# Where the vector work of a gated linear attention stage stands in its plan: mixes, gate sums, one scaling and one norm factor moved

## The chip, the cores and the metric

The kernel runs on one core of one Trainium2 chip, in one launch. The metric is the device time of that launch in microseconds (us), lower is better. The kernel computes with TensorE (PE, matrix products), VectorE (DVE), ScalarE (ACT), GpSimd (POOL) and the queue of SyncE (SP), which starts most of the transfers from memory. Each engine works through its own instructions in a fixed order and waits where an operand or a buffer is not there yet.

## The reference

Two layers over 512 positions of width 1024, all in float32. The first layer mixes by pooling and a short convolution, the second by gated linear attention; each is followed by a gated FFN with a convolution. The change lies in the attention of the second layer alone:

```python
q, k, v, r, gl = jnp.split(h, [...], axis=-1)              # h = rmsnorm(x) @ gla_w_in
g = jax.nn.log_sigmoid((gl @ w_g2 + b_g).astype(f32)) / GLA_TAU
bcum = jnp.cumsum(heads(g, GLA_HK), axis=3)                # in chunks of 64 positions
q_in = q * jnp.exp(bcum);  k_in = k * jnp.exp(-bcum)
att = jnp.where(mask, jnp.einsum('bhnlk,bhnmk->bhnlm', q_in, k_in), 0.0)
o_intra = jnp.einsum('bhnlm,bhnmv->bhnlv', att, v)
kv = jnp.einsum('bhnlk,bhnlv->bhnkv', k * jnp.exp(b_last - bcum), v)
_, states = lax.scan(step, init, (kv, decay))              # state over the chunks
o = o_intra + jnp.einsum('bhnlk,bhnkv->bhnlv', q_in, states)
o = o * lax.rsqrt(jnp.mean(o * o, axis=-1, keepdims=True) + EPS) * norm_g
o = o.reshape(bsz, s, GLA_DV) * jax.nn.silu(r)             # then @ gla_w_out, + x
```

There are four heads, with 128 columns of q and k and 256 of v and r each.

## The kernel before

**Number format.** Every matrix product is taken in three parts: each float32 operand is split into a high part (ACT copies it to a shorter format) and a low part (DVE subtracts), and PE adds high by high, high by low and low by high. So each block of weights costs a transfer into a `raw` buffer (three of them), an ACT instruction (`hi`, line 219) and a DVE instruction (`lo`, line 223) before PE can use it.

**The plan.** The attention stage is one list of steps. `at(t, fn)` puts a step at a planned time; `run_plan` sorts the steps by time and emits them, and PE, DVE and ACT then keep exactly that order. The planned times are not enforced at run time: they only set the order of each engine's queue. Transfers on SP and POOL wait for their buffers.

**The buffers.** Products land in PSUM, which has eight banks of 128x512; a bank is handed out when the program is built, and a product whose bank is still being read waits. Intermediate tiles of 128x512 come from a pool of 41 slots (`slot`).

The stage runs as follows; `t` is the planned time.

1. **v and the low-rank gate input**: `v_chunk` (lines 1063 to 1065, tile `vg`) takes the token-major products, four column blocks b = 0 to 3 with four banks each, and `v_out` (line 1069) copies each bank out. Beside b = 0 the row norm is found: `rsqrt_small` takes `v` (line 294), `y` (296), `t` (300, 301) and the result `y` (302), which the spreading product `bc` (line 328) needs on PE. Beside b = 1 the gate input is transposed (`low_rank`, `glT`), and `gate_logits` (lines 1009, 1011, tile `z`) follow: heads 0 and 1 ahead of b = 2, heads 2 and 3 in the middle of it. `log_gate`, `log_gate2` (ACT: exp and log) and `log_gate3` (DVE: line 1027 and the running sum, line 1029, tile `bc`) make the gate sums of all heads.
2. **The mixes** (`mix_parts`, `mix_in_plan`), four of them, also lie beside v. They build sums of the two halves of x for a seven-product scheme that the q and k projections use: ACT scales (`scale`, line 420), DVE takes four sums (`sums`, lines 427 to 430), ACT makes two high parts (`high`, line 435), DVE two low parts (`low`, line 440).
3. **Pairs of r and q/k**, for heads 0 to 3: `gate(i)` is the projection of r in six parts of four products (line 1274, tile `r`), then scaled by DVE (line 391) and put through Silu by ACT (line 1340). `queries_keys(h)` takes seven products p1, p2, p6, p5, p7, p3, p4 of twelve matmuls (line 562) into three banks: `stx`, `styz`, `stz`. ACT copies `stx` out between them (`keep`, line 1306), and p6 has to wait for the copy of p1's result. The piece `a2` of the weights that p3 and p4 use is split beside the products (lines 513 and 519).
4. **Head by head**: `decays` and `decays2`, `decays3` need the gate sum; `keys`, `keys2` scale q and k; `scores` (banks `att`, `kot`), `masked`, `kv`, `states` (ACT line 1143, DVE line 1145), `outputs` (two banks `o` per head, lines 1155 and 1157).
5. **Norm of a head**: `squares_of` squares both `o` banks (ACT, line 1166), adds (DVE, line 1169) and splits the sum (`nh`, ACT line 315; `nl`, DVE line 316). `head_norm` puts the total over the partitions on PE (lines 311 and 312, tile `ss`) and `out_norm` the steps after it: ACT `ny` and `nt` (318, 319), DVE `nt` (320), ACT `nt` (321), DVE `ro` (322), and the scaling `y` of both halves (line 1185), which reads the two `o` banks for the last time.
6. **Output**: `out_gate` multiplies with Silu(r) (line 1195) and splits (`yh`, ACT line 1199; `yl`, DVE line 1203). Then `mix_out` takes the output projection (line 264, tile `go`). It is not in the plan: its first two blocks start with the parts of heads 0 to 2, and the rest needs head 3's. Each of its results is added to x (line 347) and prepared for the FFN; this uses a `raw` buffer too (`xg`), so that the sixth block of weights of `go` waits for it.

r's eight projections stand at: gate(0) ahead of the first q/k pair, gate(1) to gate(3) ahead of the next, gate(4) to gate(7) behind the last, with the outputs of heads 2 and 3 between them.

Of the kernel before, what the change touches and what calls it, by code (L numbers as in the profile page):

```python
# [72 lines left out]
def trunk_kernel(ctx, tc, xT, cols, w_ab, w_pool, w_abo, w_vg, w_qk, w_r, w_g2, w_go, w_up, w_dn, w_ds, outT):  # L73
# [11 lines left out]
    def slot(dt=F32, name="s"):  # L85
        return big.tile([P, T], dt, tag="s", name=name)
# [27 lines left out]
    def col(name, i=0):  # L114
        c = COLS[name] + i
        return colt[:, c : c + 1]
# [48 lines left out]
    def f32(ap):  # L165
        return ap.bitcast(F32)
# [76 lines left out]
    done = [0]  # L243
# [81 lines left out]
    def spread_small(y, n):  # L325
        b = bank("bc")[:, : n * P]
        for c in range(n):
            PE.matmul(
                b[:, c * P : (c + 1) * P], y[:, c : c + 1].broadcast_to([P, P]), ident, start=True, stop=True
            )  # L330
        return b

    def sums(acc, c0=0, n=NTT):
        b = bank("ss")
        for c in range(n):
            PE.matmul(b[:, c : c + 1], acc[:, (c0 + c) * P : (c0 + c + 1) * P], ones[:, 0:1], start=True, stop=True)
        return b
# [121 lines left out]
    def at(t, fn):  # L459
        events.append((t, len(events), fn))  # L460
# [487 lines left out]
    total = []  # L948
# [76 lines left out]
    def log_gate3(h):  # L1025
        e, z = heads[h].pop("e"), heads[h].pop("z")
        V.scalar_tensor_tensor(z, z, 0.0, e, ALU.min, ALU.subtract)
        bc = heads[h]["bc"] = slot(name="bc")
        V.tensor_tensor_scan(bc, starts, z, 0.0, ALU.mult, ALU.add)
# [130 lines left out]
    def squares_of(h, t):  # L1160
        q = heads[h]

        def raw():
            q["sq"] = [slot(name="osq") for _ in range(2)]
            for sq, o in zip(q["sq"], q["o"]):
                S.activation(sq, o, AF.Square)

        def total():
            V.tensor_tensor(q["sq"][0], q["sq"][0], q["sq"][1], ALU.add)
            q["ro"], q["norm"] = norm_wide(q["sq"][0], 256, "ro")  # L1170

        at(t, raw)
        at(t + 1.3, total)
        ready_at = 6.5 if h < 2 else 1.7
        at(t + ready_at, lambda: q["norm"][0]())
        at(t + ready_at + (1.6 if h < 2 else 0.6), lambda: q["norm"][1]())

    def out_norm(h, t):
        q = heads[h]
        for step, after in zip(range(3, 8), (0.0, 0.7, 1.4, 2.2, 3.0)):  # L1180
            at(t + after, lambda step=step: q["norm"][step]())

        def scale(e):
            q.setdefault("y", []).append(slot(name="y"))
            V.scalar_tensor_tensor(q["y"][e], q["o"][e], col("gnorm", e), q["ro"], ALU.mult, ALU.mult)

        for e in range(2):
            at(t + 3.8 + 0.7 * e, lambda e=e: scale(e))

    def out_gate(h, e, t):  # L1190
        i = 2 * h + e

        def gate():
            y = heads[h]["y"][e]
            V.tensor_tensor(y, y, sil[i], ALU.mult)

        def high():
            y_h[i] = slot(F32R, "yh")
            S.activation(y_h[i], heads[h]["y"][e], AF.Copy)

        def low():
            y_l[i] = slot(F32R, "yl")
            V.tensor_tensor(y_l[i], heads[h]["y"][e], f32(y_h[i]), ALU.subtract)

        at(t, gate)
        at(t + 0.8, high)
        at(t + 1.5, low)

    def mix_in_plan(i, t):
        scale, sums, high, low = mix_parts(i, "mix1")  # L1210

        def done():
            mixed[i] = low()

        at(t, scale)
        at(t + 0.8, sums)
        at(t + 2.2, high)
        at(t + 3.5, done)

    t = 0.0  # L1220

    def then(us, fn):
        nonlocal t
        at(t, fn)
        t += us

    def next_block(lead=13.0, high=8.0, low=6.6):
        block(t - lead, t - high, t - low)
# [4 lines left out]
    at(0.0, lambda: V.tensor_scalar(minus_gain, colt[:, COLS["mix1"] + HK : COLS["mix1"] + KD], -1.0, None, ALU.mult))  # L1233
    mixed = [None] * HK
    for i in range(HK):
        mix_in_plan(i, 9.6 + 4.6 * i)
    first = True
    for b, (n, ks) in enumerate(zip(VG_COLS, VG_K)):
        k0 = 0
        for i, kt in enumerate(ks):  # L1240
            if b or i > 1:
                next_block()
            then(kt * 12 * n * 0.000443, lambda b=b, n=n, k0=k0, kt=kt: v_chunk(b, n, k0, kt))
            k0 += kt
            if b == 0 and i == 1:
                then(0.9, lambda: rsqrt_small(y4, sums(acc)[:, :NTT], NTT, D))
            if b == 0 and i == 2:
                then(0.9, lambda: S.activation(rs, spread_small(y4, NTT), AF.Copy))
            if b == 1 and i == 0:
                then(0.5, low_rank)  # L1250
            if (b, i) in ((1, 1), (2, 0)):
                for h in ((0, 1) if b == 1 else (2, 3)):
                    then(0.24, lambda h=h: gate_logits(h))
                    at(t + 1.5, lambda h=h: gate_sizes(h))
            if b == 2 and i == 0:
                for h in range(HEADS):
                    at(t + 2.2 + 0.1 * h, lambda h=h: log_gate(h))
                    at(t + 4.6 + 0.1 * h, lambda h=h: log_gate2(h))
                    at(t + 6.0 + 2.0 * h, lambda h=h: log_gate3(h))
        for c in range(NTT):  # L1260
            at(t + 0.1 + 0.4 * c, lambda b=b, n=n, c=c: v_out(b, n, c))

    scaled_at, sil_at = {}, {}
# [24 lines left out]
    def queries_keys(h):  # L1288
        nonlocal t
        w = seven_weights(w_qk[h], t, "gla", 2)  # L1290
        b, q = {}, {}

        def product(name):
            if not qk_ops:
                qk_ops.update(operands(mixed))
            out, first, ts = {
                "p1": ("x", True, lo_t), "p2": ("yz", True, lo_t), "p6": ("x", False, lo_t),
                "p5": ("z", True, lo_t), "p7": ("x", False, lo_t), "p3": ("yz", False, hi_t),
                "p4": ("x", False, lo_t),
            }[name]  # L1300
            seven_product(w, b, qk_ops, name, out, first, ts)

        def keep(tile, ts):
            if tile not in q:
                q[tile] = slot(name=tile)
            S.activation(q[tile][:, ts], b["x"][:, lo_t], AF.Copy)

        def add_p5(tile):
            V.tensor_tensor(q[tile][:, hi_t], b["z"][:, lo_t], q[tile][:, hi_t], ALU.add)

        def key():
            V.scalar_tensor_tensor(q["k"], q["k"], -1.0, rs, ALU.mult, ALU.mult)
            heads[h]["k"] = q["k"]

        def query():
            V.tensor_tensor(q["q"], b["yz"], q["q"], ALU.add)

        def query2():
            V.tensor_tensor(q["q"], q["q"], rs, ALU.mult)
            heads[h]["q"] = q["q"]  # L1320

        for n, name in enumerate(DOWN_SEVEN):
            at(t + n * UNIT, lambda name=name: product(name))
        at(t + 1 * UNIT + 0.1, lambda: keep("q", lo_t))
        at(t + 3 * UNIT + 0.1, lambda: keep("q", hi_t))
        at(t + 4 * UNIT + 0.2, lambda: add_p5("q"))
        at(t + 5 * UNIT + 0.1, lambda: keep("k", hi_t))
        at(t + 5 * UNIT + 0.6, lambda: add_p5("k"))
        t += 7 * UNIT
        at(t - 0.6, query)  # L1330
        at(t + 0.1, lambda: keep("k", lo_t))
        at(t + 0.15, query2)
        at(t + 0.8, key)
# [4 lines left out]
    def gate(i, between={}, split_at=(6.0, 4.8)):  # L1338
        project_into("r", i, store_r, between, split_at)
        at(t + 1.2, lambda: S.activation(sil[i], sil[i], AF.Silu))  # L1340
        sil_at[i] = t + 1.8
# [18 lines left out]
    def head_norm(h):  # L1360
        then(0.46, lambda: heads[h]["norm"][2]())
        out_norm(h, t + 0.1)
        scaled_at[h] = t + 5.4

    def gates_of(h, t):
        at(t + 2.0, lambda: decays(h))
        at(t + 1.6, lambda: decays2(h))
        at(t + 5.8, lambda: decays3(h))

    gate(0)  # L1370
    gates_of(0, t)
    queries_keys(0)
    head_keys(0, 1.6)
    gate(1, {4: lambda: head_scores(0)}, (3.6, 2.4))
    gates_of(1, t)
    queries_keys(1)
    head_kv(0)
    head_keys(1, 1.6)
# [9 lines left out]
    late = t + 2.5  # L1388
# [5 lines left out]
    head_scores(3)  # L1394
    gate(5, {4: lambda: (head_kv(3), head_norm(2))})
    gate(6, {1: lambda: head_out(3)})
    gate(7, {4: lambda: head_norm(3)})
    for h in range(HEADS):
        for e in range(2):
            out_gate(h, e, max(scaled_at[h] + 0.7 * e, sil_at[2 * h + e], late + 5.0 + 8.0 * h + 0.7 * e if h < 2 else 0.0))  # L1400
    for i in range(2):
        block(t - 8.0 + 3 * i, t - 5.0 + 2.5 * i, t - 3.8 + 2.5 * i)
    run_plan()
# [141 lines left out]
```

## Time and profile before

| | |
|---|---|
| three runs, median | 1012.91 us (1012.45 to 1013.28) |
| the profiled execution | 1013.42 us |
| its span, first to last instruction | 1011.7 us |
| mean granted TensorE clock | 0.997 |
| busy in the span: PE, DVE, ACT, POOL | 998.2, 847.1, 623.6, 69.6 us |
| the attention stage, by the timeline of PE | from 467.98 (first `vg`) to 628.42 (first `go`) |
| the output projection `go` | 628.42 to 673.48 |

In a timeline each row has the start, the time to the end of the last instruction of the row, the engine, the line, the operation, output and inputs with their shape, and the number of instructions; a bracket gives the time that the engine sat idle before it (from about 0.15 us up) and whom it waited for. Starts are in us from the start of the span. Consecutive instructions overlap a little, so the distance of two starts is shorter than the duration of the first: a DVE step of 128x512 lasts 0.69 us and takes 0.60 us of the queue.

### The profile page before, as it was taken

The numbers are of one execution on the slowest core, as the hardware profiler recorded it, in microseconds if no ns is written. First come the engines' busy times: TensorE is split into PE (matmuls) and PEld (weight loads), VectorE is DVE, ScalarE is ACT, GpSimd is POOL, SyncE is SP. The second block draws the span as 40 slices with busy tenths as digits, with TensorE's granted clock in tenths as the row PEclk, the third lists the DMA queues.
The fourth block names the chain that finished last, engine by engine and source line by source line (L and its number), as shares of the span: only waits on it lengthen the run. The fifth ranks groups of instructions, "written<-read, shape, count | busy, mean of one in ns | idle before, by whom it ended". The sixth has DMA issues, their size and how long they took to land.

```text
span 1011.7 us, 17531 instructions
## 1 busy us (share of the span) xinstructions
PE 998.2 (99%) x6996; PEld 925.4 (91%) x6996; DVE 847.1 (84%) x1224; ACT 623.6 (62%) x954; POOL 69.6 (7%) x93
## 2 busy tenths in 40 slices
PE   9999999999999999999999999999999999999996
PEld 7888889999999988899999998789999999988896
DVE  7886689999999997767868787789999999997775
ACT  6442567766766754345785767767766766764451
POOL 0001000111111000002000000100101101000000
PEclk9999999999999999999999999999999999999998
DMA  6437136787787454527325112736687787454522
GB/s 223 147 103 179 54 111 166 194 204 182 198 205 183 129 130 135 142 76 199 103 79 140 53 67 80 188 115 170 184 207 184 197 202 184 137 125 133 135 87 84
DMA packets 61267, 147.03 MB, mean 145 GB/s; under 512 B 5152, under 2 KB 7584, under 8 KB 61184
## 3 DMA queue, kind: packets, MB, share of 16 engines
q1 hardware_dynamic: 45808, 116.93, 36.2%
q0 software_dynamic: 14688, 28.32, 17.3%
q8 instruction: 55, 0.90, 0.3%
q10 hardware_dynamic: 688, 0.65, 0.2%
q14 instruction: 28, 0.23, 0.1%
HBM read 143.78 MB, written 2.10 MB: 144 GB/s over the span
## 4 chain that ended last, share of the span: by engine, by line
PE 89%; DVE 5%; ACT 4%; DMA 1%; issue 1%; SPq 0%; DVEq 0%; ACTq 0%
PE stx L562 29%; PE styz L562 18%; PE dn L264 15%; PE abo L264 4%; PE pc L264 2%; PE dn L562 2%; PE pb L264 2%; PE px L264 2%; PE go L264 2%; PE r L1274 2%; PE stz L562 2%; PE v L596 1%; PE u L596 1%; PE pu L264 1%; PE vg L1063 1%; PE vg L1065 1%
## 5 line engine op out<-in xcount | busy, mean ns | idle before, releaser
L519 DVE TENSOR_TENSOR lo<-raw,hi 128x1024 fp32r<-128x1024 f32 x108 | 131.9, 1222 | 17.4 <-ACT hi L513 17.4
L513 ACT ACTIVATE hi<-raw 128x1024 fp32r<-128x1024 f32 x108 | 114.3, 1059 | 22.5 <-PE styz L562 15.1
L223 DVE TENSOR_TENSOR lo<-raw,hi 128x1024 fp32r<-128x1024 f32 (+3 forms) x83 | 95.9, 1157 | 17.6 <-ACT hi L219 16.9
L219 ACT ACTIVATE hi<-raw 128x1024 fp32r<-128x1024 f32 (+3 forms) x83 | 83.2, 1002 | 19.2 <-DMA raw<-in_w_ab 4.8
L495 POOL DMA_DIRECT2D s<-in_w_up x42 | 50.7, 1206 | 577.4 <-ACT k L614 136.0
L380 DVE SCALAR_TENSOR_TENSOR cacc<-u,colt,cacc 128x511 f32<-128x511 f32 x96 | 71.6, 746 | 1.8 <-ACT cacc L377 1.8
L377 ACT ACTIVATE cacc<-u,colt 128x512 f32<-128x512 f32 x48 | 39.4, 821 | 45.9 <-DVE u L629 36.1
L519 DVE TENSOR_TENSOR lo<-s,hi 128x1024 fp32r<-128x1024 f32 x54 | 65.7, 1217 | 0.0
L513 ACT ACTIVATE hi<-s 128x1024 fp32r<-128x1024 f32 x54 | 57.2, 1059 | 1.1
L562 PE MATMUL stx<-th,hi 128*128 128x256 f32 x368 | 56.7, 276 | 0.0
L562 PE MATMUL stx<-th,lo 128*128 128x256 f32 x368 | 56.7, 276 | 0.0
L562 PE MATMUL stx<-tl,hi 128*128 128x256 f32 x368 | 56.7, 276 | 0.0
L264 PE MATMUL dn<-mh,hi 128*128 128x512 f32 (+1 forms) x238 | 56.5, 377 | 0.0
L264 PE MATMUL dn<-mh,lo 128*128 128x512 f32 (+1 forms) x238 | 56.4, 376 | 0.0
L264 PE MATMUL dn<-ml,hi 128*128 128x512 f32 (+1 forms) x238 | 56.4, 376 | 0.0
L562 PE MATMUL styz<-xh,lo 128*128 128x256 f32 x360 | 55.4, 276 | 0.0
L562 PE MATMUL styz<-xh,hi 128*128 128x256 f32 x360 | 55.4, 276 | 0.0
L562 PE MATMUL styz<-xl,hi 128*128 128x256 f32 x360 | 55.4, 276 | 0.0
L264 PEld LDWEIGHTS dn<-mh,lo 128*128 128x128 f32 x238 | 42.9, 188 | 8.2
L513 ACT ACTIVATE sh<-raw 128x512 fp32r<-128x512 f32 x54 | 34.3, 635 | 26.1 <-DVE raw L524 26.1
L264 PEld LDWEIGHTS dn<-ml,hi 128*128 128x128 f32 x238 | 42.9, 188 | 8.2
L264 PEld LDWEIGHTS dn<-mh,hi 128*128 128x128 f32 x238 | 42.2, 188 | 7.7
(347 smaller groups left out, 2612.8 us busy)
## 6 DMA issues: line engine op xcount, KB each, us to landing
raw<-in_w_up SPq DMA_DIRECT2D x46, 512.0 KB, 6.2
s<-in_w_up SPq DMA_DIRECT2D x42, 512.0 KB, 6.8
s<-in_w_up POOLq DMA_DIRECT2D x42, 512.0 KB, 6.4
raw<-in_w_dn SPq DMA_DIRECT2D x32, 448.0 KB, 3.3
raw<-in_w_up SPq DMA_DIRECT2D x42, 256.0 KB, 3.2
raw<-in_w_ab SPq DMA_DIRECT2D x14, 512.0 KB, 3.5
raw<-in_w_abo SPq DMA_DIRECT2D x8, 512.0 KB, 4.0
s<-in_w_ds SPq DMA_DIRECT2D x8, 512.0 KB, 6.2
```

The source lines that it names most:

```text
L219: S.activation(parts[0], raw, AF.Copy)
L223: V.tensor_tensor(parts[1], raw, f32(parts[0]), ALU.subtract)
L264: PE.matmul(out, w[:, k, :], a[k], start=first and i == 0 and k == 0, stop=last and i == 2 and k == n - 1, skip_group_check=loose,)
L377: S.activation(acc[0], u, AF.Identity, bias=col(bname, j), scale=col(wname, 2 * nj + j))
L380: V.scalar_tensor_tensor(a, u[:, : T - i], col(wname, (2 - i) * nj + j), a, ALU.mult, ALU.add)
L495: G.dma_start(w["s31"].rearrange("p (a n) -> p a n", a=2), part, accum_op=ALU.add)
L513: S.activation(h, src(), AF.Copy)
L519: V.tensor_tensor(lo, src(), f32(h), ALU.subtract)
L562: PE.matmul(b[out][:, ts], wt[:, ks[k]], a[k], start=first and i == 0 and k == 0, stop=i == 2 and k == HK - 1, skip_group_check=True,)
L596: PE.matmul(o, w[:, k, :], a[k], start=i == 0 and k == 0, stop=i == 2 and k == KD - 1)
L1063: PE.matmul(o[c][:, :n], xh[kk][:, cs], h[:, k, :], start=kk == 0, stop=False)
L1274: PE.matmul(o, w[:, k, :], a[k], start=i == 0 and k == 0, stop=k == KD - 1 and i == 5, skip_group_check=True)
```

## The change

Only planned times are altered, and with them the order in which the engines get the steps. No instruction is added, removed or altered.

- **Mixes**: the four mixes start at 7.0, 11.6, 21.0 and 25.6 in place of 9.6, 14.2, 18.8 and 23.4; inside a mix the high parts come 0.8 later and the low parts 0.7 later. In DVE's order the sums of mix 0 now stand ahead of `rsqrt_small`, the low parts of mix 0 and the sums of mix 1 ahead of the third weights block's `lo`; only the sums of mix 2 stand between `glT` and the `z` of heads 0 and 1, and mix 3's sums and low parts come behind these.
- **Gate sums**: `log_gate3` of heads 2 and 3 leaves the stretch beside b = 3. Head 2's goes behind the `decays` of head 0, ahead of `a2`'s low part in the first q/k pair; head 3's goes between the two `add_p5` of the second pair.
- **Head 0's scaling**: the step `ro` and both `y` of head 0 go 13.0 later, from among the `keys` of head 2 into the fourth q/k pair: `ro` ahead of head 1's `nl`, the first `y` ahead of `a2`'s low part, the second between the two `add_p5`.
- **Head 3's norm**: its sum and split come earlier behind its squares, its total on PE goes from behind part 4 to behind part 1 of gate(7), and with it all steps up to `yh` and `yl`. The split of gate(7)'s weights goes 4.0 earlier (on ACT ahead of head 3's `states`, on DVE behind them), and head 2's `out_gate` 4.0 later (behind head 3's `nl`).

```diff
-        at(t + 1.3, total)
-        ready_at = 6.5 if h < 2 else 1.7
+        at(t + (0.6 if h == 3 else 1.3), total)
+        ready_at = (6.5, 6.5, 1.7, 0.8)[h]
...
     def out_norm(h, t):
         q = heads[h]
-        for step, after in zip(range(3, 8), (0.0, 0.7, 1.4, 2.2, 3.0)):
+        late = 13.0 if h == 0 else 0.0
+        for step, after in zip(range(3, 8), (0.0, 0.7, 1.4, 2.2, 3.0 + late)):
...
-            at(t + 3.8 + 0.7 * e, lambda e=e: scale(e))
+            at(t + 3.8 + late + 0.7 * e, lambda e=e: scale(e))
...
-        at(t + 2.2, high)
-        at(t + 3.5, done)
+        at(t + 3.0, high)
+        at(t + 4.2, done)
...
-        mix_in_plan(i, 9.6 + 4.6 * i)
+        mix_in_plan(i, (7.0, 11.6, 21.0, 25.6)[i])
...
-                    at(t + 6.0 + 2.0 * h, lambda h=h: log_gate3(h))
+                    if h < 2:
+                        at(t + 6.0 + 2.0 * h, lambda h=h: log_gate3(h))
...
     gates_of(0, t)
+    at(t + 4.9, lambda: log_gate3(2))
...
     gates_of(1, t)
+    at(t + 7.3, lambda: log_gate3(3))
...
-    gate(7, {4: lambda: head_norm(3)})
+    gate(7, {1: lambda: head_norm(3)}, (10.0, 8.6))
...
-            out_gate(h, e, max(scaled_at[h] + 0.7 * e, sil_at[2 * h + e], ...))
+            out_gate(h, e, max(scaled_at[h] + 0.7 * e + 4.0 * (h == 2), sil_at[2 * h + e], ...))
```

More of the change, by code (lines that the diff above doesn't have):

```diff
@@ L1396, in trunk_kernel @@
     gate(6, {1: lambda: head_out(3)})
-    gate(7, {4: lambda: head_norm(3)})
+    gate(7, {1: lambda: head_norm(3)}, (10.0, 8.6))
     for h in range(HEADS):
         for e in range(2):
-            out_gate(h, e, max(scaled_at[h] + 0.7 * e, sil_at[2 * h + e], late + 5.0 + 8.0 * h + 0.7 * e if h < 2 else 0.0))
+            out_gate(h, e, max(scaled_at[h] + 0.7 * e + 4.0 * (h == 2), sil_at[2 * h + e], late + 5.0 + 8.0 * h + 0.7 * e if h < 2 else 0.0))
     for i in range(2):
```

## The prediction

> **What bounds the kernel now.** I read the page first, then the busy time by stretches of the attention stage, then the timeline of PE there for rows with a bracket, then the timelines of DVE and ACT around each of these.
>
> ```profile
> span 1011.7 us, 17531 instructions
> PE 998.2 (99%) x6996; PEld 925.4 (91%) x6996; DVE 847.1 (84%) x1224; ACT 623.6 (62%) x954; POOL 69.6 (7%) x93
> ...
> 468.00:517.00 49.00, 48.06 (x409) 47.68 (x408) 35.01 (x59) 34.95 (x57) 5.13 (x15) 1.00 0.44 121
> ...
> 571.00:594.00 23.00, 22.42 (x166) 20.98 (x166) 18.69 (x33) 16.55 (x25) 0.00 (x0) 1.00 0.19 63
> ...
> 629.00:674.00 45.00, 44.06 (x194) 35.80 (x193) 36.26 (x53) 32.47 (x46) 3.62 (x3) 1.00 0.62 164
> ```
>
> PE is busy for 99% of the span, and the change takes no matmul away. So only time in which PE waits can be won, and only in this stage: 49.00 - 48.06 = 0.94, 0.58 and 0.94 us in three stretches (length, then PE's busy time). The granted clock (third number from the end) is 1.00 in all of them. PE's timeline shows these 2.5 us as four waits:
>
> ```profile
> 498.80 0.39 PE L1063 MATMUL vg<-hi,xh 128*128 128x256 f32 x1 [0.94 <-DVE z L1011]
> 587.00 0.74 PE L562 MATMUL stx<-th,sh 128*128 128x256 f32 x4 [0.58 <-ACT q L1306]
> 639.82 1.19 PE L264 MATMUL go<-yh,hi 128*128 128x512 f32 x4 [0.36 <-ACT yh L1199]
> 657.02 2.11 PE L264 MATMUL go<-yh,hi 128*128 128x512 f32 x8 [0.58 <-ACT hi L219]
> ```
>
> Their sum is 0.94 + 0.58 + 0.36 + 0.58 = 2.46 us, 0.24% of the time. That is the most that the change can win, apart from losses too short for a bracket. Everything else is what it adds.
>
> **Mixes, the wait at 498.80.** PE needs a bank that the DVE step `z` frees; `z` stood late in DVE's queue.
>
> ```profile
> 478.43 0.15 DVE L294 TENSOR_SCALAR v<-ss 128x4 f32<-128x4 f32 x1
> ...
> 479.30 0.16 DVE L302 SCALAR_TENSOR_TENSOR y<-t,y 128x4 f32<-128x4 f32 x1
> 479.52 0.43 DVE L427 TENSOR_TENSOR ta<-xg 128x256 f32<-128x256 f32 x1
> ...
> 481.17 1.22 DVE L223 TENSOR_TENSOR lo<-raw,hi 128x1024 fp32r<-128x1024 f32 x1
> ...
> 495.08 0.43 DVE L427 TENSOR_TENSOR ta<-xg 128x256 f32<-128x256 f32 x1 [0.87 <-ACT xg L420]
> ...
> 497.99 1.41 DVE L1011 TENSOR_SCALAR z<-z,colt 128x512 f32<-128x512 f32 x2
> ...
> 480.88 1.05 PE L328 MATMUL bc<-ident,y 128*128 128x128 f32 x8
> ```
>
> Ahead of `z` stand the sums of mix 3 (from 495.08, 1.65 as below), an idle 0.87, and mix 2's two low parts (about 1.2). All of these leave, 3.7 us; `z` starts near 494.3, as soon as its product is there. The wait lasts 0.94, so it goes: **-0.94**.
>
> The price lies at the other end. The sums of mix 0 now stand ahead of `v`. Four sums take 479.52 to 481.17 = 1.65 us. The result `y` (L302) ended at 479.30 + 0.16 = 479.46 and now ends at 481.11. PE's spreading product `bc` started at 480.88 without a wait. From the end of `z` (497.99 plus half of 1.41 = 498.70) to the matmul that it released (498.80) is a hand-over of 0.10. So `bc` starts at 481.22: **+0.34**. It would cost nothing if the sums ran earlier, but DVE is taken until 478.43 by steps that stay; it can't cost more than 1.65. The later steps of mixes 0 and 1 then stand ahead of `gl` and `lo`, by my count up to 0.3 us before PE asks; I take nothing.
>
> **Gate sums.** Each is two DVE steps, one of 128x512 (0.6 in the queue) and the running sum, some 1.8 us.
>
> ```profile
> 515.40 1.22 DVE L1029 TENSOR_TENSOR_SCAN bc<-starts,z 128x512 f32<-128x512 f32 x1
> ...
> 528.20 1.23 DVE L519 TENSOR_TENSOR lo<-raw,hi 128x1024 fp32r<-128x1024 f32 x1 [2.43 <-ACT hi L513]
> ...
> 559.09 0.69 DVE L1169 TENSOR_TENSOR osq<-osq 128x512 f32<-128x512 f32 x1 [2.36 <-ACT osq L1166]
> ```
>
> Head 2's falls into the idle 2.43 before 528.20, which covers it. Head 3's finds no such hole where it stands; it pushes keys and weights of the second pair back by 1.1 to 1.8 us until the idle 2.36 before 559.09 takes it up. The `outputs` and `scores` between start at 555 and later, at least 2 us after what they need. Cost and gain: 0. They hold three more slots for a while; I count 38 of 41 at the peak, as before.
>
> **Head 0's scaling, the wait at 587.00.**
>
> ```profile
> 578.15 0.69 DVE L322 TENSOR_TENSOR ro<-nt,ny 128x512 f32<-128x512 f32 x1
> 578.87 1.41 DVE L1185 SCALAR_TENSOR_TENSOR y<-o,colt,ro 128x512 f32<-128x512 f32 x2
> 580.19 0.42 DVE L1098 TENSOR_TENSOR kb<-ka,bc 128x256 f32<-128x256 f32 x1
> ...
> 585.33 0.67 DVE L391 TENSOR_TENSOR r<-r,rs 128x512 f32<-128x512 f32 x1
> ...
> 580.71 0.60 ACT L1166 ACTIVATE osq<-o 128x512 f32<-128x512 f32 x1 [0.96 <-PE o L1157]
> ...
> 586.58 0.37 ACT L1306 ACTIVATE q<-stx 128x256 f32<-128x256 f32 x1
> ...
> 589.44 0.69 DVE L316 TENSOR_TENSOR nl<-osq,nh 128x512 fp32r<-128x512 f32 x1 [1.70 <-ACT nh L315]
> 590.66 1.23 DVE L519 TENSOR_TENSOR lo<-raw,hi 128x1024 fp32r<-128x1024 f32 x1 [0.53 <-ACT hi L513]
> ...
> 592.13 0.62 PE L562 MATMUL styz<-xh,lo 128*128 128x256 f32 x4
> ```
>
> From 578.15 to 580.19 go 2.04 us out of DVE's queue. Not all of it reaches `r` (L391), since two ACT steps after the squares (580.71) now limit; I get 0.66 us, `r` at 584.67, and the copy `q` that PE waited for ends near 586.3 in place of 586.95. PE was ready at 587.00 - 0.58 = 586.42. **-0.58**.
>
> The three steps come back in the fourth pair, where DVE sat idle for 1.70 and 0.53. `ro` and one `y` fit; that `y` stands ahead of `lo` of `a2`, which would then end at 591.4, while p3's last part wants it at 592.13 - 0.58 = 591.55. I take 0; the far end is one `y`, 0.7.
>
> **Head 3's norm, the wait at 639.82.** The total moves three parts of r ahead, to 624.0 by the old times (622.19 and eight products of 0.227).
>
> ```profile
> 614.24 0.37 ACT L1143 ACTIVATE st<-kv 128x256 f32<-128x256 f32 x1
> 614.63 1.28 ACT L318 ACT_TABLE_LOAD   x1
> 615.92 0.69 ACT L318 ACTIVATE ny<-ss,eps_t 128x512 f32<-128x512 f32 x1
> ...
> 619.74 1.05 ACT L219 ACTIVATE hi<-raw 128x1024 fp32r<-128x1024 f32 x1
> ...
> 620.60 1.41 DVE L1185 SCALAR_TENSOR_TENSOR y<-o,colt,ro 128x512 f32<-128x512 f32 x2
> ...
> L315 ACT ACTIVATE nh<-osq x2: 634/634/635, 609.2 to 625.8; 128x512 fp32r<-128x512 f32 x2
> ...
> 622.19 1.98 PE L1274 MATMUL r<-xh,hi 128*128 128x512 f32 x8
> ...
> 626.73 0.40 PE L311 MATMUL ss<-nh,ones_r 128*128 128x512 f32 x1
> 627.18 0.50 PE L312 MATMUL ss<-nl,ones_r 128*128 128x512 f32 x1
> 627.52 1.07 PE L1274 MATMUL r<-xh,lo 128*128 128x512 f32 x4
> ```
>
> Does its operand come in time? gate(7)'s `hi` (619.74; 1.05, of which 0.95 of the queue) moves ahead of `st` on ACT, so head 2's whole chain is 0.95 later: both `y` of head 2 end at 622.87 in place of 621.92. Then come the sum (0.60), `nh` (0.63) and `nl` (0.69): `nl` ends at 624.94, the second matmul of the total starts at 625.0, and the next part of r at 625.25. Without a wait it would start at 624.0 + 0.46 = 624.46: 0.79 lost. Before, 626.73 to 627.52 was 0.79 for 0.46, so 0.33 was lost already. **+0.46**; from below -0.33, if `nl` is early, and from above 1.3 with the states of head 3 late as well, whose `st` I find just in time (614.24 + 0.95 + 0.37 = 615.56). From there to `yh` the chain is over 1.5 us ahead of need, so the wait at 639.82 goes: **-0.36**.
>
> On this chain ACT changes its function table twice. The next ACTIVATE (615.92) starts 0.01 after the load's 1.28. The Trainium skill, "ScalarE: Activation LUTs", section "What ACT_TABLE_LOAD costs", counts a further 1380 ns of drain for every switch; by it `nl` would be some 2.8 us later, a rival below. The trace disagrees.
>
> **The wait at 657.02.** It hangs on a chain:
>
> ```profile
> 648.74 7.09 DMA raw<-in_w_go
> 655.91 1.07 ACT hi L219
> ```
>
> The transfer waits for a `raw` buffer that the first results of `go` occupy. Before `yh` arrived PE did twelve matmuls of later blocks first (2.7 us). With `yh` over 1.5 us early I expect the first result ahead of most of these, and the transfer with it: **-0.58**. If that order of PE stays, it is 0.
>
> **Sum.** -0.94 + 0.34 - 0.58 + 0.46 - 0.36 - 0.58 = -1.66 us. The profiled execution took 1013.42 (span 1011.7 and 1.7 around it), so 1011.76; on the median of 1012.91, half a us lower, 1011.25, say **1011.2**. A measurement of this kernel can tell about 0.2% (2.03 us) from no change: below 1010.9 is faster, above 1014.9 slower.
>
> **Rivals.**
> A. *The two new waits don't arise*: DVE reaches `v` and `nl` sooner than I count. Then up to 2.46, with the 0.33 at the total up to 2.8: about 1010.4. For it: both are sums of ten or more rows and miss by tenths. Against: `v`'s is short arithmetic.
> B. *The gains at `go` stay out*: PE's order there is fixed when the program is built, and the wait at 657.02, perhaps also 639.82, remains: -1.66 + 0.94 = -0.72, 1012.2.
> C. *PSUM, the slower side*: head 0's two banks are held 10 us or more longer. Around 584 two banks for head 0, two for head 1, `r`, `att`, `kot` and `stx` make eight of eight. If p5 of the fourth pair is handed a bank of head 0, PE waits from 588.1 until the first `y`, 590.2: 2.1 plus hand-over. Net -1.66 + 2.2 = +0.5: 1013.4. It decides as soon as that bank is chosen instead of one of the two free ones. For it: at 498.80 the bank chosen was one freed late. Against: two others are free by then. Struck at a second place it passes 2.03.
> D. *The table switches cost the drain*: head 3's total waits 2.8 longer, +1.1: 1014.0, by the row above nearly excluded.
>
> **How the numbers follow.** Forecast 43% (its own range 1010.8 to 1012.0), A 20%, B 22%, C 12%, D 3%. Faster: A and a sixth of the forecast, 27%. Slower: half of C and a little of D, 7%. The rest, 66%, is within 0.2%. From 1010.2 (A) to 1013.4 (C) holds 8 in 10.
>
> **What would show it.** Right: no bracket at the `vg` after `z`, none at p6 of the fourth pair; one of about 0.3 us at `bc`, and about 0.8 us between the total's first matmul and the next part of r in gate(7). Wrong: a bracket at `styz` of the fourth pair released by `a2`'s `lo`, at `stz` released by `y` L1185 (C), at `outputs` of head 3 released by `st`, or the wait at 657.02 unchanged (B). What stays outside 468 to 674 should not change.

## The result and the profile after

The changed kernel takes **1010.91 us** (median of 16 runs, 1010.03 to 1012.21) beside 1012.67 for the kernel before in as many runs on the same chip (1011.60 to 1014.65): a ratio of 0.9982, 95% interval 0.9974 to 0.9990. That is 1.76 us or 0.17% less: the interval leaves out 1, so the gain is real, but it is inside the 0.2% that the prediction took for no change. A repeat later on gave 1011.40 (11 runs) beside 1012.78 (15 runs), again 0.9982, 0.9973 to 0.9991. The profiled execution took 1010.67, its span is 1009.0. First its page:

```profile
span 1009.0 us, 17529 instructions
...
PE 998.1 (99%) x6996; PEld 926.5 (92%) x6996; DVE 847.0 (84%) x1224; ACT 621.9 (62%) x954; POOL 69.5 (7%) x93
```

PE does the same 998 us of work in a span that is 2.7 shorter, so what went is waiting. (The two instructions fewer are semaphore waits.) The busy time in the stretches of the attention stage (length first, then PE's):

```profile
468.00:517.00 49.00, 49.00 (x411) 48.41 (x410) 35.51 (x58) 36.47 (x61) 4.07 (x15) 1.00 0.44 127
571.00:594.00 23.00, 23.00 (x168) 21.49 (x167) 18.40 (x32) 17.20 (x27) 0.00 (x0) 1.00 0.23 79
594.00:629.00 35.00, 34.75 (x190) 29.60 (x189) 27.81 (x47) 24.11 (x36) 0.00 (x0) 1.00 0.19 63
629.00:674.00 45.00, 44.67 (x197) 36.36 (x196) 38.60 (x56) 31.37 (x45) 3.62 (x3) 1.00 0.61 155
```

The 0.94 and 0.58 of the first two stretches are gone, a 0.25 has come up in the third, and 0.33 of the 0.94 in the last is left. The timeline of PE shows them as two waits. The row at 584.16 is the p6 that waited 0.58 before; it has no bracket now:

```profile
584.16 0.73 PE L562 MATMUL stx<-th,sh 128*128 128x256 f32 x4
...
621.40 0.50 PE L311 MATMUL ss<-nh,ones_r 128*128 128x512 f32 x1
622.13 0.50 PE L312 MATMUL ss<-nl,ones_r 128*128 128x512 f32 x1 [0.22 <-DVE nl L316]
622.47 0.87 PE L1276 MATMUL r<-xl,hi 128*128 128x512 f32 x3
...
653.85 1.43 PE L264 MATMUL go<-yh,hi 128*128 128x512 f32 x5 [0.33 <-ACT hi L219]
```

To see what each step is worth, I take the starts of PE's instructions behind the first `vg` of the stage, in us. Such distances go by starts alone, while a bracket depends on the modelled end of the matmul before it. The last column, the first product of the FFN (line 596, or 611 where `xg` lies in slots), ends the stage.

| kernel | `bc` | `z` of heads 2, 3 | first `r` | total of head 1 | total of head 2 | `go` | stage |
|---|---|---|---|---|---|---|---|
| before | 12.90 | 32.31 | 49.11 | 125.97 | 144.06 | 160.44 | 205.50 |
| after | 12.91 | 31.16 | 47.96 | 124.24 | 142.33 | 159.27 | 203.42 |
| mixes alone | 12.95 | 31.40 | 48.20 | 125.40 | 143.49 | 159.88 | 204.03 |
| gate sums alone | 12.90 | 32.32 | 49.12 | 126.05 | 144.14 | 160.53 | 205.13 |
| head 0 alone | 12.90 | 32.28 | 49.08 | 125.27 | 143.36 | 159.76 | 203.89 |
| head 3 alone | 12.90 | 32.29 | 49.10 | 125.94 | 144.03 | 161.00 | 205.00 |
| total behind part 2 | 13.31 | 31.94 | 48.74 | 125.03 | 143.12 | 159.25 | 203.71 |
| two mixes' sums ahead of `v` | 14.47 | 32.71 | 49.51 | 125.72 | 143.81 | 160.73 | 204.78 |
| `xg` in slots | 13.09 | 31.34 | 48.14 | 124.39 | 142.48 | 159.36 | 202.88 |
| head 0 five us later still | 13.19 | 31.44 | 48.24 | 124.49 | 142.58 | 159.78 | 203.30 |
| after, second profile | 13.27 | 31.51 | 48.31 | 124.57 | 142.66 | 159.61 | 203.72 |
| total and mask moved | 12.90 | 31.07 | 47.87 | 124.09 | 142.18 | 158.36 | 202.55 |
| the same and `xg` in slots | 12.90 | 31.08 | 47.88 | 124.08 | 142.17 | 158.28 | 202.02 |

Between the first two profiles the stage is 2.08 shorter. The span shrank by 2.7; the rest is not the change's. The part ahead of the stage is 1.10 shorter: the first product `pc` of the first layer already starts at 30.38 before and at 29.25 after, and in the other profiles anywhere from 29.25 to 30.24, with the same code up to there. The part behind the stage is 0.42 longer (338.25 and 338.67; 338.1 to 338.9 in the other profiles), none of it up to the FFN's last projection `dn`, which starts 211.60 behind the end of the stage in both.

### The profile page after: what moved, and what is told of

Read it like the earlier page. It is cut to its first block, busy times and chain, and to the rows that moved or that the text cites. A ratio compares the mean times of both kernels' runs of the same rounds, so it can differ in the third digit from the quotient of the medians.

```text
span 1009.0 us, 17529 instructions
## 1 busy us (share of the span) xinstructions
PE 998.1 (99%) x6996; PEld 926.5 (92%) x6996; DVE 847.0 (84%) x1224; ACT 621.9 (62%) x954; POOL 69.5 (7%) x93
## 4 chain that ended last, share of the span: by engine, by line
PE 94%; DVE 2%; ACT 2%; DMA 1%; issue 0%; SPq 0%; DVEq 0%; ACTq 0%
PE stx L562 29%; PE styz L562 18%; PE dn L264 15%; PE abo L264 4%; PE go L264 3%; PE r L1276 3%; PE pc L264 2%; PE pb L264 2%; PE px L264 2%; PE dn L562 2%; PE stz L562 2%; PE vg L1063 1%; PE vg L1065 1%; PE vg L1064 1%; PE v L596 1%; PE u L596 1%
## 5 line engine op out<-in xcount | busy, mean ns | idle before, releaser
L562 PEld LDWEIGHTS stx<-tl,hi 128*128 128x128 f32 x368 | 48.6, 188 | 0.0
```

The lines of the kernel that those rows point to most:

```text
L562: PE.matmul(b[out][:, ts], wt[:, ks[k]], a[k], start=first and i == 0 and k == 0, stop=i == 2 and k == HK - 1, skip_group_check=True,)
```

## The experiments

**One part at a time.** The theory was the sum of the prediction; its rivals were that the two new waits stay away (A) and that the order of PE at `go` keeps both waits there (B). Four kernels each make one part of the change alone. These and the next four kernels were each timed once, so I give the time but argue by the starts in the table. Mixes:

```diff
-        at(t + 2.2, high)
-        at(t + 3.5, done)
+        at(t + 3.0, high)
+        at(t + 4.2, done)
...
-        mix_in_plan(i, 9.6 + 4.6 * i)
+        mix_in_plan(i, (7.0, 11.6, 21.0, 25.6)[i])
```

> Before with the mixes' new times alone. Measured is the stage from the first vg matmul to the first matmul of the second FFN (v, line 596): 205.50 us before, 203.42 after. Theory 'each part for itself': the wait of vg for z goes, with its true length of 1.1 us (start to start) and not the 0.94 of its bracket: stage 204.3 to 204.4; spreading product bc 12.9 to 13.25 us behind the first vg, by how early POOL's second transfer lets DVE go on. Rival 'the parts need each other' (the gate sums must leave the queue for the mixes to pay): stage above 205.0.

Measured: 1011.61 (before on that chip 1012.97). The wait for `z` is gone: from the `z` of heads 0 and 1 to that of heads 2 and 3 it is 5.92 in place of 7.16, so 1.24, though the bracket had said 0.94. `bc` starts 0.05 late and its first matmul takes 0.07 more than before, so that 0.12 is lost there and not 0.34. But `go` starts only 0.56 earlier. The missing 0.6 lies in two stretches in which no wait ends. The second is seen in the windows view, first this kernel, then the one before, over the same 62 matmuls of the second q/k pair:

```profile
541.20:548.49 7.29, 7.29 (x62) 7.29 (x61) 4.04 (x7) 5.47 (x8) 1.20 (x1) 1.00 0.56 170
```

```profile
542.40:549.26 6.86, 6.86 (x62) 6.86 (x61) 3.77 (x6) 5.43 (x8) 1.05 (x1) 1.00 0.56 181
```

PE is busy throughout and takes 6% longer for the same matmuls: their starts lie 0.120 us apart in place of 0.113, at a granted clock that the column gives as 1.00. The other stretch, from 481.8 to 487.3, is of the same kind (0.118). What causes them is open. No other profile has the second one; the kernel with the total behind part 2 shows the first again, from 481.5 to 493.1. Without them the part is worth 1.2. The stage came out at 204.03, under the 204.3 foretold in spite of them, because in this profile the wait for `hi` at `go` does not arise (the transfers are compared below).

Gate sums:

```diff
-                    at(t + 6.0 + 2.0 * h, lambda h=h: log_gate3(h))
+                    if h < 2:
+                        at(t + 6.0 + 2.0 * h, lambda h=h: log_gate3(h))
...
+    at(t + 4.9, lambda: log_gate3(2))
...
+    at(t + 7.3, lambda: log_gate3(3))
```

> Before with the gate sums of heads 2 and 3 moved alone. Theory 'each part for itself': 0, stage 205.4 to 205.6, since both fall into idle time of DVE. Rival 'the parts need each other': it alone already makes r of the first pair earlier and shows a gain or loss of over 0.3 us.

Measured: 1013.00, and all starts up to `go` within 0.1 of before. Cost and gain are nothing, or a tenth of cost, as forecast. The stage, 205.13, is under the 205.4 foretold because of a shorter transfer at `go` (below), not because of this step.

Head 0's scaling:

```diff
+        late = 13.0 if h == 0 else 0.0
...
-            at(t + 3.8 + 0.7 * e, lambda e=e: scale(e))
+            at(t + 3.8 + late + 0.7 * e, lambda e=e: scale(e))
```

> Before with head 0's scaling moved alone. Theory 'each part for itself': p6 of the fourth pair no longer waits for the copy of q; true length of that wait 0.74 (start to start), 0.66 after the short handover that stays: stage 204.8 to 204.9. Rival 'PSUM' (a bank of head 0 is chosen for a product of the fourth pair): a new wait of about 2 us at stx, styz or stz there, stage 206 or more. Rival 'the parts need each other': 205.3 or more.

Measured: 1012.06. The total of head 1 starts 0.70 earlier, `go` 0.68; no wait for a bank appears. The stage, 203.89, is 0.9 under the 204.8 foretold: from `go` on it took 44.13 in place of 45.06, as the wait for `hi` does not arise here either.

Head 3's norm:

```diff
-        at(t + 1.3, total)
-        ready_at = 6.5 if h < 2 else 1.7
+        at(t + (0.6 if h == 3 else 1.3), total)
+        ready_at = (6.5, 6.5, 1.7, 0.8)[h]
...
-    gate(7, {4: lambda: head_norm(3)})
+    gate(7, {1: lambda: head_norm(3)}, (10.0, 8.6))
...
-            out_gate(h, e, max(scaled_at[h] + 0.7 * e, sil_at[2 * h + e], late + 5.0 + 8.0 * h + 0.7 * e if h < 2 else 0.0))
+            out_gate(h, e, max(scaled_at[h] + 0.7 * e + 4.0 * (h == 2), sil_at[2 * h + e], late + 5.0 + 8.0 * h + 0.7 * e if h < 2 else 0.0))
```

> Before with head 3's norm moved alone (with the earlier split for gate(7) and head 2's later output). Theory 'each part for itself': the total waits 0.5 to 0.6 us for nl, the wait for yh (true 0.52) goes, and the rest at go depends on one transfer's landing (7.1 us before, 6.9 after): stage 205.1 to 205.5. Rival 'order of go' (PE's order there has changed so that the first result comes earlier): the wait of go for hi is gone, stage 204.6. Rival 'the parts need each other': over 205.7, since the total meets PE without the gains ahead of it.

Measured: 1012.47. `go` starts 0.56 later, the price at the total. The wait for `yh` is gone, the wait for `hi` is 0.17 by its bracket, and from `go` to the end of the stage it takes 44.00 in place of 45.06. By its starts 0.34 of the wait for `hi` is left, so the rival by which it goes is out.

The parts add up. Up to `go`: -1.2 (mixes, without the two stretches) + 0.1 - 0.7 + 0.6 = -1.2; all together -1.17.

**The price at `bc`.** Why did mix 0's sums ahead of `v` cost next to nothing? DVE's timeline of the changed kernel at the head of the stage:

```profile
474.55 0.72 DVE L1231 CAST mask<-maskf 128x512 int32<-128x512 f32 x1 [2.28 <-POOL maskf L967]
...
478.60 0.16 DVE L294 TENSOR_SCALAR v<-ss 128x4 f32<-128x4 f32 x1
...
479.48 0.16 DVE L302 SCALAR_TENSOR_TENSOR y<-t,y 128x4 f32<-128x4 f32 x1
```

and PE's:

```profile
479.66 0.29 PE L1065 MATMUL vg<-lo,xh 128*128 128x272 f32 x1
479.79 0.46 PE L328 MATMUL bc<-ident,y 128*128 128x128 f32 x2
```

`y` ends at 479.64, and `bc` starts 0.15 behind it, at 479.79, which is only 0.01 later than before (12.91 and 12.90 in the table). Its first matmul takes 0.18 up to the next, where it took 0.11 before; with that 0.09 is lost. All of DVE's queue here hangs on the copy of the mask, which waits for POOL. In the kernel before it stood at 476.02:

```profile
476.02 0.72 DVE L1230 CAST mask<-maskf 128x512 int32<-128x512 f32 x1 [3.47 <-POOL maskf L967]
```

That is 8.04 behind the first `vg` (467.98), against 7.67 after (474.55 - 466.88). POOL makes `maskf` only after its second transfer of `s`, which waits for the first to land. POOL's timeline, before and after:

```profile
472.46 1.20 POOL L495 DMA_DIRECT2D s<-in_w_qk  x1 [3.32 <-DMA s<-in_w_qk]
...
475.24 0.75 POOL L967 TENSOR_SCALAR_AFFINE_SELECT maskf<-maskf 128x512 f32<-128x512 f32 x1
```

```profile
471.00 1.20 POOL L495 DMA_DIRECT2D s<-in_w_qk  x1 [2.92 <-DMA s<-in_w_qk]
...
473.77 0.75 POOL L967 TENSOR_SCALAR_AFFINE_SELECT maskf<-maskf 128x512 f32<-128x512 f32 x1
```

So a landing 0.4 earlier may have hidden a price that is there. The test puts one more mix's sums ahead of `v`:

```diff
-        mix_in_plan(i, (7.0, 11.6, 21.0, 25.6)[i])
+        mix_in_plan(i, (7.0, 7.3, 21.0, 25.6)[i])
```

> The changed kernel with mix 1's steps 4.3 us earlier in the plan, so that the sums of two mixes stand ahead of v on DVE. If bc hangs on DVE's queue ahead of v as the prediction says (and only escaped in the changed kernel because the mask copy, which waits for a landing, was 0.37 us earlier), y ends four sums later, 1.65, and bc starts about 1.5 us later: 14.4 behind the first vg instead of 12.91; stage 204.9 or more. If PE is bound at bc by its own matmuls and the sums ahead of v cost nothing, bc stays at 12.9 and the stage at 203.4.

Measured: 1012.12 (before on that chip 1012.41), stage 204.78. DVE's and PE's timelines show the second set of sums, `v`, `y`, and `bc` with its wait:

```profile
478.65 0.41 DVE L427 TENSOR_TENSOR ta<-xg 128x256 f32<-128x256 f32 x1
...
480.29 0.15 DVE L294 TENSOR_SCALAR v<-ss 128x4 f32<-128x4 f32 x1
...
481.17 0.16 DVE L302 SCALAR_TENSOR_TENSOR y<-t,y 128x4 f32<-128x4 f32 x1
```

```profile
481.48 0.79 PE L328 MATMUL bc<-ident,y 128*128 128x128 f32 x5 [1.40 <-DVE y L302]
```

`bc` starts 1.57 late. PE does hang on `y`, and sums ahead of `v` cost nearly what they take (1.57 of 1.65).

A second profile of the changed kernel was foretold from this:

> The changed kernel itself, unchanged, on the same chip as c1 and c2, to compare with them directly, and a second profile of it. If the start of bc hangs on the mask copy, bc starts 5.24 behind the mask copy's start (12.90 at the earliest), whatever that is here, between 12.9 and 13.3; the part from go to v between 43.5 and 44.5 with the length of the sixth block's transfer (6.0 to 7.1). If the two were accidents of one profile, both come out as in the first one, 12.91 and 44.15, with another start of the mask copy and another length of the transfer. Ratio to before 0.9975 to 0.9990.

Measured: the mask copy and `y` on DVE, and `bc` on PE:

```profile
475.49 0.72 DVE L1231 CAST mask<-maskf 128x512 int32<-128x512 f32 x1 [3.46 <-POOL maskf L967]
...
480.41 0.16 DVE L302 SCALAR_TENSOR_TENSOR y<-t,y 128x4 f32<-128x4 f32 x1
```

```profile
480.72 0.46 PE L328 MATMUL bc<-ident,y 128*128 128x128 f32 x2 [0.20 <-DVE y L302]
```

With the first `vg` at 467.45 the copy is at 8.04, as in the profile of before, and `bc` at 13.27: 0.37 late, where the prediction had 0.34 for that landing. In the six profiles in which mix 0's sums alone stand ahead of `v` the copy started at 7.67, 7.72, 7.85, 7.96, 8.04, 8.07 and `bc` at 12.91, 12.95, 13.09, 13.19, 13.27, 13.31: always 5.23 or 5.24 behind the copy. On the mean `bc` starts 0.22 late; its first matmul takes 0.07 more in all six, so 0.29 is lost on the mean and 0.44 in this profile. From `go` to the end of the stage it took 44.11 with a transfer of 6.77, too near the first profile (44.15 and 6.85) to say anything about that wait.

**The total of head 3.** Does it cost because `nl` is late, or because it stands inside gate(7) at all?

```diff
-    gate(7, {1: lambda: head_norm(3)}, (10.0, 8.6))
+    gate(7, {2: lambda: head_norm(3)}, (10.0, 8.6))
```

> The changed kernel with head 3's total behind part 2 of gate(7) instead of part 1, eight matmuls later. Stage = first vg to first v of L596 on PE; changed kernel 203.42. If the total waits because DVE's nl is late (the step of +0.46 in the prediction, 0.56 measured up to go), both its matmuls now follow each other at 0.23 us and go starts 0.5 earlier: 158.75 behind the first vg instead of 159.27; stage 202.9. The rival that the loss is the price of the total standing inside gate(7) at all (its weights are ones, not weights of the gate) keeps 0.79 between its first matmul and the next part of r: go at 159.3, stage 203.4. A third way: the factor is later by the one or two hi that now stand ahead of nt on ACT, yh of the first result comes 1.5 to 2 us later and PE waits at go for yh: go at 158.75, but stage 203.2 to 203.6.

Measured: 1011.02, stage 203.71, not 202.9. Up to the total of head 2 this profile is 0.79 later than the changed kernel's first one: `bc` starts 0.40 later, and one of the slower stretches follows (481.5 to 493.1, 0.41 in all). So I read the part alone: from the total of head 2 to `go` it is 16.13, after 16.94, before 16.38. The total waits for `nl`, and eight matmuls later it does not: its two matmuls follow each other at 0.24. Even the 0.33 that before lost there is mostly gone. But a little is lost again at `go`, where PE now comes to head 3's first `yh` just as it gets ready (ACT, then PE):

```profile
636.57 1.23 ACT L1200 ACTIVATE yh<-y 128x512 fp32r<-128x512 f32 x2 [2.31 <-DVE y L1196]
```

```profile
634.48 3.97 PE L264 MATMUL go<-yh,hi 128*128 128x512 f32 x16
638.28 0.40 PE L264 MATMUL go<-yl,hi 128*128 128x512 f32 x1
```

Sixteen matmuls at 0.227 take 3.63, and the next row starts 3.80 on: 0.17 is lost, too short for a bracket. Inside the row the first matmul that needs `yh` starts 0.05 late, at 637.25, and the next follows it after 0.34. That is the third way of the expectation, at its edge: counted from the total of head 2, this `yh` is 1.1 later than in the changed kernel. From `go` on it took 44.46, with 0.45 at the `hi` (bracket).

**The wait for the sixth weights block.** The chain that ended last, in the changed kernel:

```profile
645.80 6.85 DMA raw<-in_w_go
...
652.74 1.07 ACT hi L219
...
653.85 16.61 PE go L264 x72
```

The forecast was that PE takes the first result ahead of most of the twelve matmuls of later blocks, and that the transfer starts sooner with it. PE's order at `go` did not change like that. The run of high by high products ahead of head 3's first `yl` is one of 15 matmuls now (the first row) where it was one of 16 before, 12 and, behind the wait for `yh`, 4 (the second row and the one at 639.82 in the prediction):

```profile
634.31 3.56 PE L264 MATMUL go<-yh,hi 128*128 128x512 f32 x15
```

```profile
636.58 2.88 PE L264 MATMUL go<-yh,hi 128*128 128x512 f32 x12
```

In both the first result is complete with the 57th matmul of `go`. The transfer does start sooner, 19.65 behind the first `go` in place of 20.32, since the wait for `yh` is gone from the time before it. But it is gone from PE's way to the sixth block as well: PE is there 27.2 behind the first `go` in place of 27.9, its wait for `hi` left out. So nothing is won at `hi`. The transfer and the wait, from all eleven profiles with this buffer (length from issue to landing; the wait is the distance of two matmul starts less their usual one):

| kernel | transfer | wait |
|---|---|---|
| before | 7.09 | 0.74 |
| total behind part 2 | 6.97 | 0.61 |
| after | 6.85 | 0.49 |
| total and mask moved | 6.79 | 0.43 |
| after, second profile | 6.77 | 0.41 |
| two mixes' sums ahead | 6.75 | 0.40 |
| head 3 alone | 6.69 | 0.34 |
| gate sums alone | 6.63 | 0.28 |
| mixes alone | 6.24 | 0 |
| head 0 five us later still | 6.10 | 0 |
| head 0 alone | 5.86 | 0 |

In every row with a wait it is the length less 6.35 (to within 0.01), with head 3's total in its old place and in a new one, and in the rows without one the length is below that. The lengths overlap too: 5.86 to 7.09 in the old place, 6.10 to 6.97 in a new one. So the wait follows the transfer, and no effect of the change on it is seen; what makes one transfer longer than another is open. To see that the buffer makes the chain, one kernel keeps the products `xg` in slots, so that the block needs no `raw` buffer from the first result:

```diff
     def mix_tokens(i, gname):
+        if gname == "ffn1":
+            xa, xb = slot(name="xa"), slot(name="xb")
+            S.activation(xa, x[i], AF.Copy, scale=col(gname, i))
+            S.activation(xb, x[i + HK], AF.Copy, scale=col(gname, i + HK))
...
```

> The changed kernel with the products xg of the second layer's mixes in two slots instead of in a buffer of raw, so that the sixth weight block of go needs no buffer that the first result of go frees. If the wait at the first matmul of that block hangs on this buffer (chain: first result, xall, xh, xg, ta, tb, transfer, hi), the bracket there goes and the part from go to v takes 43.65 us instead of 44.15; stage 202.9. If it hangs on the transfer's own length under load or on ACT's queue, the wait stays at 0.3 to 0.6 and the stage at 203.2 to 203.6.

Measured: 1010.31; from `go` to the end of the stage 43.52, no wait for `hi`. But PE now comes to the next stage before its operand (its timeline, the first products of the FFN, line 611 in this kernel):

```profile
671.76 0.50 PE L611 MATMUL v<-xh,hi 128*128 128x512 f32 x1 [0.27 <-ACT xh L280]
```

Part of the gain is given back there, to a wait that the earlier one had hidden.

**The banks.** How near was rival C? Head 0's scaling goes five us later still:

```diff
-        late = 13.0 if h == 0 else 0.0
+        late = 18.0 if h == 0 else 0.0
```

> The changed kernel with head 0's factor and scaling 5 us later still (18 instead of 13), behind the query and key steps of the fourth pair, so that head 0's two banks are held about 5 us longer. If there are free banks, as the prediction took it, PE starts everything up to the total of head 1 as before and the stage stays at 203.4, at most 0.2 more for states of the next head that move behind a y on DVE. If the banks are the bound (rival C, just not reached at 13), PE waits at kv or at r of the next part for the first y, 1.5 to 3 us: stage 205 to 206.4.

Measured: 1010.34, stage 203.30. The scaling on DVE reads the last bank of head 0 from 594.92 on, where the changed kernel does so at 589.34:

```profile
593.66 0.74 DVE L1186 SCALAR_TENSOR_TENSOR y<-o,colt,ro 128x512 f32<-128x512 f32 x1
...
594.92 0.74 DVE L1186 SCALAR_TENSOR_TENSOR y<-o,colt,ro 128x512 f32<-128x512 f32 x1
```

PE's waits in the whole stage, as the view of waits gives them:

```profile
PE ss L312 <- DVE nl L316: 0.2, 1, 0.2
```

No bank is waited for, so C was over 5 us off. What it costs is 0.3 at the outputs of head 3, whose states DVE makes 0.3 later behind the total of head 2, too short for a bracket. From `go` on it took 43.52, since the transfer took 6.10 and no wait for `hi` arose.

**Both remedies together.** The runs point to a better kernel: the total behind part 2, and the copy of the mask, which nothing needs until the scores of head 0, behind the sums of mix 1, so that DVE's head no longer hangs on POOL:

```diff
-    at(1.0, lambda: V.tensor_copy(mask, maskf))
+    at(12.6, lambda: V.tensor_copy(mask, maskf))
...
-    gate(7, {1: lambda: head_norm(3)}, (10.0, 8.6))
+    gate(7, {2: lambda: head_norm(3)}, (10.0, 8.6))
```

> The changed kernel with two edits: the copy of the mask on DVE moved from the head of the stage to behind the sums of mix 1, and head 3's total behind part 2 of gate(7). If bc starts 0.31 behind y's start and y 4.93 behind the mask copy, as in six runs so far, y no longer hangs on the landing behind the mask, comes some 0.6 earlier, and bc starts at 12.90 behind the first vg whatever the landings do (0.01 to 0.41 less than in the runs with the sums ahead of v). The total costs 0.5 to 0.8 less up to go: 158.5 for go where the changed kernel had 159.27. Stage 202.6 to 202.9 if the transfer of the sixth block is as long as in the changed kernel's profile; about 0.8 us, 0.1%, under the changed kernel; against before a ratio of 0.9972 to 0.9976. The rival: the copy in its new place holds back lo and gl, glT waits 0.3 to 0.6, and the gain at bc is given back.

Measured: **1009.67** (1009.09 to 1010.53, 6 runs), ratio to before 0.9966, 0.9953 to 0.9978, so over 0.2% less; the changed kernel in the same series 1011.40 (1010.36 to 1012.26). That is 1.7 by medians, more than the 0.8 foretold, which was reckoned from the profile in which `bc` lost only 0.09. In the profile `bc` starts at 12.90 and the stage takes 202.55, 1.17 less than in the second profile of the changed kernel; where the other half us of the medians comes from the profiles do not show. The total on PE, without a wait, and the wait that is left:

```profile
622.21 0.40 PE L311 MATMUL ss<-nh,ones_r 128*128 128x512 f32 x1
622.45 0.40 PE L312 MATMUL ss<-nl,ones_r 128*128 128x512 f32 x1
622.69 1.09 PE L1276 MATMUL r<-xl,hi 128*128 128x512 f32 x4
...
653.20 2.11 PE L264 MATMUL go<-yh,hi 128*128 128x512 f32 x8 [0.27 <-ACT hi L219]
```

> The kernel c1 with the products xg of the second layer's mixes in slots as well. Part from go to v 43.5 instead of 44.15 and 44.46, then a wait of 0.3 to 0.5 for the last xh at v, as in the run with the slots alone, since the last result of go reaches PE's next stage through xall and xh and was hidden by the wait before. First v of L596 form at 202.0 to 202.3; net against c1 0.2 to 0.4 us less: against before a ratio of 0.9968 to 0.9974. If the slots cost elsewhere (the loads of the next stage, now spread out earlier, collide with those of go), c2 comes out level with c1 or above.

Measured: 1009.58 (1008.73 to 1010.13, 5 runs), ratio 0.9964, 0.9951 to 0.9977. The stage is 202.02, 0.53 less than without the slots, and no wait is left in it that has a bracket. From `go` on it took 43.74 where 43.5 was foretold, and the wait for `xh` at the first products of the FFN, also foretold, did not come. By the time the two can't be told apart.

## Why the prediction was right, and where it was not

1011.2 was forecast, 1010.91 came, inside the range and inside the forecast's own; 1.66 less than before was forecast, 1.76 less was measured. Step by step, in us; the third column is the pair of profiles, the fourth what the other runs say:

| step | predicted | before to after | the runs |
|---|---|---|---|
| wait for `z` | -0.94 | -1.24 | -1.24 (mixes alone) |
| `bc` waits for `y` | +0.34 | +0.09 | +0.09 to +0.48, mean 0.29 |
| gate sums | 0 | 0 | up to +0.1 |
| p6 of the fourth pair | -0.58 | -0.65 | -0.7 (head 0 alone) |
| total of head 3 | +0.46 | +0.56 | +0.56 (head 3 alone) |
| `go` waits for `yh` | -0.36 | -0.63 | 0.55 to 0.63 in the four profiles that have the wait |
| `go` waits for `hi` | -0.58 | -0.25 | follows the transfer, not the change |
| sum | -1.66 | -2.12 | about -1.6 |

The stage shrank by 2.08 between the two profiles; the 0.04 to the sum is spread in smaller pieces. The mechanisms of `z`, p6, the total and `yh` were right. At the total the prediction had 0.79 lost, all of it ahead of the second matmul. In the profile 0.80 is lost, 0.19 of it already ahead of the first matmul, which starts just behind the end of `nh` (621.35), a wait that the prediction did not have. With the 0.33 lost there before that makes 0.47; the rest of the 0.56 up to `go` is in pieces of hundredths. Of the signs it named, the bracket at `bc` is missing in the first profile and 0.20 in the second. The sum was met in part by luck, by two errors that cancel, the first two of these three:

- **The step that failed is the last one.** "With `yh` over 1.5 us early I expect the first result ahead of most of these" did not happen; for the wait at `hi` rival B was right. PE takes the first result behind as many matmuls as before, and what the wait for `yh` gave back moved the transfer and PE alike. The wait shrank only because this transfer was 0.24 shorter than in the profile of before (6.85 and 7.09). Since the wait is the length less 6.35 wherever head 3's total stands, I now count 0 for the step.
- **The gains that did come were mis-sized, all to the same side.** A bracket begins at the modelled end of the matmul before. At `go` that is 0.39 after its start, while without a wait the next one starts after 0.227. At the wait for `yh` the starts lie 0.52 further apart than usual where the bracket says 0.36, and the first matmul after the wait takes 0.11 more than its like. So a bracket of 0.36 cost 0.63, and one of 0.94 cost 1.22 (1.11 and 0.11). At p6 the extra 0.11 is there without the wait too, and only 0.65 was to be won. The Trainium skill, "Perfetto Trace Analysis", section "Tensor Engine Instruction (MATMUL, LD_WEIGHTS)", says that PE's end times are estimated from the instruction's size and not observed; the trace agrees in so far as the next matmul starts 0.227 after one that the profile has running for 0.39.
- **The price at `bc`** was about right for the landing in the profile of before. In the first profile after it was nearly missing because POOL's transfer landed sooner, as rival A had it, but by luck: in the second profile, with the copy where it was before, `bc` starts 0.37 late and 0.44 is lost; most of the difference to 0.34 is the dearer first matmul, which the prediction left out. The prediction treated DVE's queue as full "until 478.43 by steps that stay" and did not ask what the first of these steps, the mask copy, waits for.

Rival C was far off: no bank in the stage is waited for even 5 us later. Rival D finds nothing: the second matmul of the total waits 0.22 by its bracket, not 2.8.

## What to carry to other kernels

Price a wait by the distance of two starts in PE's timeline, not by its bracket, and look whether the next matmul is dearer too. Before a wait is credited to a change, follow it back to what it hangs on: where a landing stands at the head of the chain, take several profiles and plot the wait against the landing, since two profiles alone showed a gain at `hi` and next to no price at `bc`, and both were accidents. A step whose operand comes from another engine late (the mask copy) belongs behind work that is ready, because a queue that keeps its order passes the wait on to everyone behind it (here `bc` came 5.23 or 5.24 us behind the copy in six profiles of six).

## What the runs showed of the hardware

One transfer of the same block took 5.86 to 7.09 us in eleven profiles of kernels that differ in little but order, and the wait at its end was the length less 6.35 to within 0.01 in the eight that had one. In two profiles (mixes alone, total behind part 2) PE ran stretches of 5 to 12 us with its matmuls 4 to 6% further apart (0.118 or 0.120 in place of 0.113 us), without a wait and with a granted clock shown as 1.00; they cost up to 0.43 us each (7.29 for 6.86). And the first matmul after a wait was dearer than its like, by 0.07 us at `bc` and by 0.11 us at the other waits on PE in the stage; at p6 it was so without a wait too.
